# Down-projection of a gated MLP in a transformer block on one core: the weight blocks move to the queue of the left blocks, two buffer pools move, and the results get eight single-bank tiles

## The chip, the cores and the metric

One core of one Trainium2 chip runs the whole program. The metric is the device time of one execution in microseconds (us), the median of three runs. Engines are called PE (TensorE, matmuls), DVE (VectorE), ACT (ScalarE), POOL (GpSimd) and SP (SyncE, which here only issues transfers).

## The reference, cut to what matters

One layer with 1024 tokens and a width of 1024: a token mixer, a layer norm, a gated MLP with a hidden width of 2816, and a second layer norm.

```
def conv_gated_mlp(h, w_up, conv_w, conv_b, w_down):
    u = jnp.einsum('btd,df->btf', h, w_up)
    ...
    uc = conv_b + sum(conv_w[j] * up[:, j:j + T] for j in range(CONV_WIDTH))
    a, v = jnp.split(uc, 2, axis=-1)
    return jnp.einsum('btf,fd->btd', jax.nn.gelu(a) * v, w_down)
...
    h = layer_norm(ALPHA * h + mix, ln1_g[l], ln1_b[l])
    ffn = conv_gated_mlp(h, w_up[l], conv_w[l], conv_b[l], w_down[l])
    h = layer_norm(ALPHA * h + ffn, ln2_g[l], ln2_b[l])
```

## The kernel before, in words

Every large product is made of three matmuls (`mm3`, L83 to L85): each operand is split into a high part, rounded by ACT, and the rest, subtracted by DVE (`split`, L65 and L66). The parts go to buffers of the pool `wp` (five pairs). Both MLP products use a scheme of seven block products in place of eight.

**Up-projection.** `pair(f)` makes the seven products of one pair of filter tiles (f = 0 to 21) in two PSUM units of two banks, `post(f)` the convolution, the gate and the sums of gated blocks, which `store` writes to the DRAM tensors `gd`. Pair j = 10 is the last one (f = 20 and 21). `prep(f)` splits the weights; the split of its block `s1` lies in one pair of tiles `w1h`, `w1l`.

**Down-projection.** `plan` lists 42 steps: seven passes in the order P1, P2, P6, P5, P7, P3, P4, each of NS = 6 steps (five with two row blocks of 128, one with one). A full step is 4 results x 2 blocks x 3 = 24 matmuls of 128x512, a pass is 132. The left operand of step n is a gated block, loaded back from `gd` by `load_a(n)` into one of the three buffers of `rawp` (tile `rawa`, L769, on SP). The right operand is a block of `w_down` or a sum of such blocks. The 24 blocks come in the order of `w_loads` (L847): first those of P1, then those of P2, and so on; `load_w2` (L852) issues four at first and two in each step, on POOL's queue. For P1's first two steps the block goes through `rawp` as well (`rawb`, L797). `prepare(n)` splits both operands; `slot` says where the split goes: to `wp`, or to the three pairs of the second operand pool `dn` (tiles `dh`, `dl`).

P6 builds its right operands in a tile `t2` (L806, one buffer) from blocks changed in place by P2 (L818); L811 and L820 change blocks for later passes. The residual adds ALPHA times the layer norm's output: `residual(t)` loads a stored row block `zd[t]` to a tile `zn` (L857, two buffers), scales it (L858) and adds it to the result `z[t]` (L859). It is called in the passes P5 and P3, and L859 needs what P6 or P7 left in `z[t]`.

Pools on the left side of SBUF are stacked: `bigp` (`bh`, `bl`: operands of the up-projection), `tpp`, then `ugp` (buffers `ca`, `cv` of `post`); `uap` is on the right side. The down-projection's pools take their place: `zq` on the left (weight tiles, `z`, then `zn` and `t2`), `dn` on the right. With `reuse_waits="tile"` a new tile waits for the old tiles under it, without it for all of the old pool. The order of the instructions on each engine is not the written one: the framework plans it, and puts later instructions ahead where it deems earlier ones not yet ready. Slots of one tag are handed out in written order.

Results: `cs` are units of two banks from the same PSUM pool `ps` as before; P1, P6, P7 and P4 add up in `banks[1]` (four results in two units), P2, P5 and P3 in `banks[3]`. `finish` adds them to `z`. In P4 the results 0 and 1 run together, then 2, then 3; `norm2` makes the second layer norm of each row block, in the form "added" with ACT and an accumulating transfer on POOL, in the form "whole" with two DVE instructions of full width (L479, L483).

Of the kernel before, what the change touches and what calls it, by code (L numbers as in the profile page):

```python
# [9 lines left out]
F32 = mybir.dt.float32  # L10
F32R = mybir.dt.float32r
# [6 lines left out]
P = 128  # L18
T = 1024
D = 1024  # L20
# [6 lines left out]
NF = DFF // P  # L27
# [15 lines left out]
def block_kernel(ctx: ExitStack, tc: tile.TileContext, x, xT, w_ct, w_i, pool_w, w_out, w_up, w_down, pk, rows, masks, ident, out):  # L43
    nc = tc.nc
    V, A, G, PE = nc.vector, nc.scalar, nc.gpsimd, nc.tensor

    const = ctx.enter_context(tc.tile_pool(name="const", bufs=1))
    lnp = ctx.enter_context(tc.tile_pool(name="lnp", bufs=1))
    small = ctx.enter_context(tc.tile_pool(name="small", bufs=4))
    rawp = ctx.enter_context(tc.tile_pool(name="rawp", bufs=3))  # L50
    wp = ctx.enter_context(tc.tile_pool(name="wp", bufs=5))
    ps = ctx.enter_context(tc.tile_pool(name="ps", bufs=4, space=bass.MemoryType.PSUM))

    def unit():
        return ps.tile([P, 1024], F32, tag="u", name="u")
# [8 lines left out]
    def split(r, h, l):  # L64
        A.activation(out=h, in_=r, func=AF.Copy)  # L65
        V.tensor_tensor(out=l, in0=r, in1=h.bitcast(F32), op=ALU.subtract)  # L66

    def wpair():
        return wp.tile([P, 1024], F32R, tag="wh", name="wh"), wp.tile([P, 1024], F32R, tag="wl", name="wl")
# [10 lines left out]
    halves, whole = [slice(0, 512), slice(512, 1024)], slice(0, 1024)  # L80
# [293 lines left out]
    for lv in range(NL):  # L374
        G.tensor_copy(out=maskt[:, lv, :].rearrange("p (c t) -> p c t", t=P),
                      in_=mraw[:, lv * P:(lv + 1) * P].rearrange("p (o t) -> p o t", o=1).broadcast_to([P, 4, P]))
# [32 lines left out]
    tmp = [hg.tile([P, 1024], F32, name=f"tmp{j}") for j in range(2)]  # L409
    pb = [tmp[0], sets[0][1], sets[0][2]]  # L410
# [3 lines left out]
    for j in range(4, 16):  # L414
        while len(ahead) < 3 and j + len(ahead) < 16:
            ahead.append(weight(w_ct[j + len(ahead)]))
        w = ahead.pop(0)
# [14 lines left out]
    for h in range(NH):  # L432
        for e in range(2):
# [5 lines left out]
    jps = [(j, j + 1) if j + 1 < NF // 2 else (j,) for j in range(0, NF // 2, 2)]  # L439
    gd = {(n, i): tc.dram_tile([P, len(js), 512], F32, name=f"gd{n}{i}")  # L440
          for n in ("11", "12", "22", "s1", "s2", "s3", "s4") for i, js in enumerate(jps)}
# [14 lines left out]
    def row(i, tag):  # L456
        r = lnp.tile([P, D], F32, tag=tag, name=f"row{i}")
        nc.sync.dma_start(out=r, in_=rows[i:i + 1, :].broadcast_to([P, D]))
        return r
# [26 lines left out]
    def stats(zt, c, st6):  # L486
        V.bn_stats(out=st6[:, c.start // 512, :], in_=zt[:, c])
# [84 lines left out]
    def raw_up(i):  # L572
        if i not in raws:
            raws[i] = raw(w_up[i])
        return raws[i]
# [29 lines left out]
    ua = uap.__enter__()  # L605
    ops, outs = {}, {}
    lo, hi = halves

    def parts(w):
        return [[e[:, c] for e in w] for c in halves]  # L610

    def prep(f):
        ra, rv = raw_up(f), raw_up(NF + f)
        w = wpair()
        split(ra, *w)
        o = ops[f] = {}
        o["11"], o["12"] = parts(w)
        yield


        s1 = ua.tile([P, 512], F32, tag="s1", name="s1")
        V.tensor_tensor(out=s1, in0=rv[:, lo], in1=rv[:, hi], op=ALU.add)
        V.tensor_tensor(out=rv[:, lo], in0=ra[:, lo], in1=rv[:, lo], op=ALU.add)
        yield
        V.tensor_tensor(out=ra[:, lo], in0=s1, in1=ra[:, lo], op=ALU.add)
        V.tensor_tensor(out=ra[:, hi], in0=ra[:, lo], in1=ra[:, hi], op=ALU.add)
        yield
        w = wpair()
        split(ra, *w)
        o["s2"], o["s4"] = parts(w)  # L630
        yield
        w = wpair()
        split(rv, *w)
        o["s3"], o["22"] = parts(w)
        yield
        o["s1"] = [ua.tile([P, 512], F32R, tag=f"w1{n}", name=f"w1{n}", bufs=1) for n in "hl"]
        split(s1, *o["s1"])

    def prod(o, w, b, start, stop):
# [51 lines left out]
    gated = {}  # L691

    def store(n, j, src):
        nc.sync.dma_start(out=gd[n, j // 2][:, j % 2, :], in_=src)

    def post(f):
        a, v = outs.pop(f)
# [30 lines left out]
    def step(gens, n=1):  # L728
        for i in range(n):
            for g in gens:  # L730
                next(g, None)

    preps = [prep(f) for f in range(NF)]
    step(preps[:2])
    norm1(u7, 7, halves)
# [14 lines left out]
    p = post(0)  # L750
# [9 lines left out]
    NS = len(jps)  # L760
# [10 lines left out]
    def w_view(r, q, c):  # L771
        b = w_down[2 * jps[q][0] + r]
        return bass.AP(tensor=b.tensor, offset=b.offset + c.start, ap=[[1024, P], [2 * P * 1024, len(jps[q])], [1, 512]])

    def w_block(r, q, c):
        return ww[r][q][:, :, c]
# [9 lines left out]
    def split2(src, n, k):  # L786
        h, l = [t[:, :k] for t in slot(n)]
        split(src, h, l)
        return h, l

    def prepare(n):
        i, q = plan[n]
        k = len(jps[q])
        a = split2(raw_a.pop(n)[:, :k, :], 2 * n, k)
        if i == P1 and q < 2:
            src = rawp.tile([P, 2, 512], F32, tag="raw", name="rawb")[:, :k]
            nc.sync.dma_start(out=src, in_=w_view(0, q, lo))  # L797
        elif i == P1:
            src = w_block(0, q, lo)
        elif i == P2:  # L800
            src = w_block(1, q, lo)
            w11 = w_block(0, q, lo)
        elif i == P6:
            w21, w22 = w_block(1, q, lo), w_block(1, q, hi)
            src = zq.tile([P, 2, 512], F32, tag="t2", name="t2")[:, :k]
            V.scalar_tensor_tensor(out=src, in0=w_block(0, q, lo), scalar=-1.0, in1=w22, op0=ALU.mult, op1=ALU.subtract)  # L806
        elif i == P5:
            src = w_block(0, q, lo)
        elif i == P7:
            src = w_block(0, q, hi)  # L810
            V.tensor_tensor(out=src, in0=w_block(1, q, hi), in1=src, op=ALU.subtract)  # L811
        elif i == P3:
            src = w_block(1, q, hi)
        else:
            src = w_block(1, q, lo)
        opsd[n] = a, split2(src, 2 * n + 1, k)
        if i == P2:
            V.tensor_tensor(out=w11, in0=w11, in1=w_block(0, q, hi), op=ALU.subtract)  # L818
        elif i == P6:
            V.tensor_tensor(out=w21, in0=w21, in1=src, op=ALU.add)  # L820
# [16 lines left out]
    tpp.__exit__(None, None, None)  # L837
    bigp.__exit__(None, None, None)
    uap.__exit__(None, None, None)
    zq = ctx.enter_context(tc.tile_pool(name="zq", bufs=1, reuse_waits="tile"))  # L840
    dn = ctx.enter_context(tc.tile_pool(name="dn", bufs=3, side="right", reuse_waits="tile"))
    ww = [[zq.tile([P, len(js), D], F32, tag=f"w{r_}{q}", name=f"w{r_}{q}") for q, js in enumerate(jps)] for r_ in range(2)]
    z = [zq.tile([P, D], F32, name=f"z{t}") for t in range(NC)]
    g1, b1_ = row(0, "g"), row(1, "b")
    st6 = maskt[:, 0, :NC * 48].bitcast(F32).rearrange("p (t a b) -> p t a b", a=2, b=6)

# [2 lines left out]

    def load_w2(n):  # L850
        for r_, q, c in w_loads[:n]:
            G.dma_start(out=w_block(r_, q, c), in_=w_view(r_, q, c))  # L852
        del w_loads[:n]

    def residual(t):
        zn = zq.tile([P, D], F32, tag="zn", name="zn", bufs=2)
        nc.sync.dma_start(out=zn, in_=zd[t])  # L857
        V.scalar_tensor_tensor(out=zn, in0=zn, scalar=ALPHA, in1=g1, op0=ALU.mult, op1=ALU.mult)  # L858
        V.tensor_tensor(out=z[t], in0=z[t], in1=zn, op=ALU.add)  # L859

    cs = [unit() for i in range(2)]
    banks = {1: [cs[p // 2][:, halves[p % 2]] for p in range(4)]}
    fresh = {P1: 1, P2: 3, P5: 3, P4: 1}
    where = {P1: 1, P6: 1, P7: 1, P4: 1, P2: 3, P5: 3, P3: 3}

# [34 lines left out]
    def norm2(t, c, how):  # L900
        stats(z[t], c, st6[:, t])
        layer_norm(z[t], g2, b2, st6[:, t], how, out[t * P:(t + 1) * P, :])


    beside = []
    prepared = 1
    load_w2(4)

    def advance(n):
        nonlocal prepared  # L910
        while prepared <= n and prepared < len(plan):
            if prepared not in raw_a:
                load_a(prepared)
            prepare(prepared)
            prepared += 1
            if prepared < len(plan) and prepared not in raw_a:
                load_a(prepared)
            load_w2(2)

    for n in range(6 * NS):  # L920
        i, q = plan[n]
        if n == NS:
            cs += [unit() for e in range(2)]
            banks[3] = [cs[2 + p // 2][:, halves[p % 2]] for p in range(4)]
        advance(n + 1)
        multiply(n, range(4))
        if q == NS - 1:
            for p in range(4):
                finish(i, p)
            if i == P6:  # L930
                beside += [lambda t=t: (residual(t), stats(z[t], lo, st6[:, t])) for t in range(4)]
            elif i == P7:
                beside += [lambda t=t: (residual(t), stats(z[t], hi, st6[:, t])) for t in range(4, 8)]
        elif beside:
            beside.pop(0)()
            if i == P3 and not beside:
                g2, b2 = row(2, "g"), row(3, "b")
# [8 lines left out]
    for q in range(NS):  # L946
        multiply(n0 + q, (2,))
    for p in range(2):
        norm2(4 + p, lo, "added")
    finish(P4, 2)  # L950
    for q in range(NS):
        multiply(n0 + q, (3,))
# [66 lines left out]
```

## Time and profile before

| | |
|---|---|
| median of 3 runs | 1058.08 us (1058.04 to 1058.32) |
| the profiled execution | 1058.64 us, span 1056.6 us, so 2.0 us lie around the span |
| PE busy | 1026.0 us, 97% of the span |
| DVE, ACT, POOL busy | 812.4, 437.8, 62.0 us |
| granted TensorE clock, mean | 0.988 |

Matmuls follow each other every 0.23 us at the full clock, though each record is 0.39 us long (they are pipelined). PE is busy nearly throughout, so the few stretches where it is not are what to look for.

### The profile page before, as it was taken

To read this page: it belongs to the slowest core of one execution; us is meant where nothing else is said; L and a number is where in the kernel's file an instruction comes from. 1 tells how busy PE (TensorE), PEld (TensorE's weight loads), DVE (VectorE), ACT (ScalarE), POOL (GpSimd) and SP (SyncE) were. 2 spreads that over 40 slices of the span, in tenths; PEclk is the share of its full clock that TensorE was granted. 3 is DMA by queue.
4 is the path that set the end of the run, shared out by engine and by line. 5 is a ranking of instruction groups with operands and counts; after the bars stand their busy time and mean duration, and the time that the engine had idled before them with its cause. 6 is when DMAs were issued, how large, how long until landed. Compare 5 with 4: busy or idle time off the path is not lost.

```text
span 1056.6 us, 12003 instructions
## 1 busy us (share of the span) xinstructions
PE 1026.0 (97%) x4680; PEld 839.2 (79%) x4680; DVE 812.4 (77%) x973; ACT 437.8 (41%) x542; POOL 62.0 (6%) x96
## 2 busy tenths in 40 slices
PE   9999999999999999999999999999999399999996
PEld 6888888888888877888778877887877388888884
DVE  6485498967745689988888987987986579795885
ACT  6421453223723375544443444444434233334441
POOL 2000000001100000000000000000000320000033
PEclk9999999999999999999999999999999799999998
DMA  8200211100142223224214323322233982352448
GB/s 323 90 20 1 80 40 41 40 1 20 41 179 100 100 100 120 100 70 140 100 61 139 100 85 115 100 99 102 100 105 133 370 307 82 108 181 98 134 126 239
DMA packets 39944, 118.62 MB, mean 112 GB/s; under 512 B 4432, under 2 KB 5328, under 8 KB 39888
## 3 DMA queue, kind: packets, MB, share of 16 engines
q1 hardware_dynamic: 35680, 103.11, 27.7%
q0 software_dynamic: 4064, 14.68, 4.5%
q8 instruction: 37, 0.61, 0.2%
q14 instruction: 19, 0.16, 0.0%
q10 hardware_dynamic: 144, 0.07, 0.0%
HBM read 89.27 MB, written 28.57 MB: 112 GB/s over the span
## 4 chain that ended last, share of the span: by engine, by line
PE 92%; DVE 3%; DMA 3%; ACT 2%; issue 0%; SPq 0%; POOL 0%; POOLq 0%; DVEq 0%; ACTq 0%
PE u L83 29%; PE u L85 29%; PE u L84 29%; PE u L228 3%; DMA zn<-zd 1%; DMA gd<-ca 1%; PE u L268 1%; PE u L270 1%; PE u L257 1%; DMA hg<-in_xT 1%; ACT hq L520 1%; DMA raw<-in_w_up 1%; DVE wl L66 1%; ACT fh L520 0%; PE u L529 0%
## 5 line engine op out<-in xcount | busy, mean ns | idle before, releaser
L83 PE MATMUL u<-bh,wh 128*128 128x512 f32 x520 | 205.6, 398 | 1.3 <-ACT ua L660 0.7
L84 PE MATMUL u<-bl,wh 128*128 128x512 f32 x520 | 202.9, 390 | 1.0 <-DVE bl L66 1.0
L85 PE MATMUL u<-bh,wl 128*128 128x512 f32 x520 | 202.9, 391 | 0.0
L65 ACT ACTIVATE wh<-raw 128x1024 fp32r<-128x1024 f32 x85 | 88.6, 1057 | 113.1 <-PE u L84 81.3
L66 DVE TENSOR_TENSOR wl<-raw,wh 128x1024 fp32r<-128x1024 f32 x85 | 103.0, 1225 | 25.7 <-ACT wh L65 23.2
L83 PEld LDWEIGHTS u<-bh,wh 128*128 128x128 f32 x520 | 97.6, 188 | 28.1 <-DVE uv L678 5.6
L85 PEld LDWEIGHTS u<-bh,wl 128*128 128x128 f32 x520 | 97.6, 188 | 21.0
L84 PEld LDWEIGHTS u<-bl,wh 128*128 128x128 f32 x520 | 97.7, 188 | 20.8 <-DVE bl L66 1.6
L83 PE MATMUL u<-th,wh 128*128 128x512 f32 x264 | 104.8, 397 | 0.0
L85 PE MATMUL u<-th,wl 128*128 128x512 f32 x264 | 103.3, 391 | 0.8 <-DVE wl L66 0.8
L84 PE MATMUL u<-tlo,wh 128*128 128x512 f32 x264 | 103.3, 391 | 0.0
L65 ACT ACTIVATE wh<-rawa 128x1024 fp32r<-128x1024 f32 (+1 forms) x30 | 30.1, 1002 | 91.6 <-PE u L84 74.9
L83 PEld LDWEIGHTS u<-th,wh 128*128 128x128 f32 x264 | 49.5, 188 | 15.8 <-ACT ua L667 3.2
L85 PEld LDWEIGHTS u<-th,wl 128*128 128x128 f32 x264 | 49.6, 188 | 12.3 <-DVE wl L66 1.2
L83 PE MATMUL u<-wh,bh 128*128 128x512 f32 x144 | 57.8, 401 | 0.0
L84 PEld LDWEIGHTS u<-tlo,wh 128*128 128x128 f32 x264 | 49.6, 188 | 9.7
L687 DVE SCALAR_TENSOR_TENSOR cv<-uv,pkt,cv 128x1023 f32<-128x1023 f32 (+1 forms) x44 | 56.1, 1276 | 0.3 <-ACT cv L685 0.2
L85 PE MATMUL u<-wh,wl 128*128 128x512 f32 x144 | 56.2, 391 | 0.0
L84 PE MATMUL u<-wl,wh 128*128 128x512 f32 x144 | 56.2, 390 | 0.0
L85 PE MATMUL u<-wh,bl 128*128 128x512 f32 x144 | 56.2, 390 | 0.0
L687 DVE SCALAR_TENSOR_TENSOR ca<-ua,pkt,ca 128x1023 f32<-128x1023 f32 (+1 forms) x44 | 56.1, 1276 | 0.0
L83 PE MATMUL u<-wh 128*128 128x512 f32 x144 | 56.1, 390 | 0.0
(216 smaller groups left out, 1978.7 us busy)
## 6 DMA issues: line engine op xcount, KB each, us to landing
raw<-in_w_up SPq DMA_DIRECT2D x42, 512.0 KB, 4.2
w<-in_w_down POOLq DMA_DIRECT2D x20, 512.0 KB, 6.0
rawa<-gds SPq DMA_DIRECT2D x20, 512.0 KB, 3.3
gd<-ca SPq DMA_DIRECT2D x33, 256.0 KB, 2.7
rawa<-gd SPq DMA_DIRECT2D x15, 512.0 KB, 4.6
raw<-in_w_ct SPq DMA_DIRECT2D x13, 512.0 KB, 3.2
gds<-sm SPq DMA_DIRECT2D x22, 256.0 KB, 2.6
gds<-ca SPq DMA_DIRECT2D x22, 256.0 KB, 4.2
```

Of the source, the lines that this page charges most:

```text
L65: A.activation(out=h, in_=r, func=AF.Copy)
L66: V.tensor_tensor(out=l, in0=r, in1=h.bitcast(F32), op=ALU.subtract)
L83: PE.matmul(o, lhsT=ah, rhs=bh, start=start, stop=False, **kw)
L84: PE.matmul(o, lhsT=ah, rhs=bl, start=False, stop=False, **kw)
L85: PE.matmul(o, lhsT=al, rhs=bh, start=False, stop=stop, **kw)
L228: PE.matmul(ul[:, p * P:(p + 1) * P], lhsT=km[:, p * P:(p + 1) * P], rhs=view(QF, p * P + hh, [2 * hh, 64 // hh], [512 - hh, 2], [1, hh]), ...
L257: PE.matmul(up[:, c * P:(c + 1) * P], lhsT=KTr[:, c * P:(c + 1) * P], rhs=vchunk(c, hs), start=True, stop=True)
L268: PE.matmul(uo[:, cs], lhsT=vchunk(c, hs), rhs=sc[:, cs], start=True, stop=c == 0)
L270: PE.matmul(uo[:, cs], lhsT=S[:, (c - 1) * P:c * P], rhs=QF[:, cs], start=False, stop=True)
L520: A.activation(out=o[:, ks], in_=u[:, ks], func=AF.Identity, scale=pkt[:, PK_LN + k:PK_LN + k + 1], bias=pkt[:, PK_LN + KT + k:PK_LN + KT ...
L687: V.scalar_tensor_tensor(out=c[:, 2 - j:], in0=u[:, :T - 2 + j], scalar=pkt[:, cw + j:cw + j + 1], in1=c[:, 2 - j:], op0=ALU.mult, op1=ALU ...
```

## The change

It moves the transfers of the weight blocks (`load_w2`) from POOL's to SP's queue, where they stand behind the `rawa` loads of their step. It moves the seven stores of the last pair (j = 10) from SP's to POOL's queue. The pool `dn` goes to the left side, ahead of `zq`, over the old `bh`. In `zq` the tiles `z` move ahead of the last two weight tiles, and `zn` and `t2` become one tag `tmp` with three buffers. The PSUM pool `ps` is closed, and a new pool `pb`, which waits for all of the old one, gives eight single-bank results. From f = 2 on, the split of `s1` goes to the two tiles `g` and `b` of the pool `lnp` in turn, where the rows `g1`, `b1_` of the first layer norm are loaded afterwards. Row blocks 4 and 5 get the form "whole" of the second layer norm.

```diff
@@ -49,7 +49,8 @@
-    ps = ctx.enter_context(tc.tile_pool(name="ps", bufs=4, space=bass.MemoryType.PSUM))
+    psp = tc.tile_pool(name="psp", bufs=4, space=bass.MemoryType.PSUM)
+    ps = psp.__enter__()
@@ -633,7 +634,11 @@
-        o["s1"] = [ua.tile([P, 512], F32R, tag=f"w1{n}", name=f"w1{n}", bufs=1) for n in "hl"]
+        if f < 2:
+            o["s1"] = [ua.tile([P, 512], F32R, tag=f"w1{n}", name=f"w1{n}", bufs=1) for n in "hl"]
+        else:
+            t = lnp.tile([P, 2, 512], F32R, tag="gb"[f % 2], name="w1")
+            o["s1"] = [t[:, 0, :], t[:, 1, :]]
@@ -691,7 +696,7 @@
-        nc.sync.dma_start(out=gd[n, j // 2][:, j % 2, :], in_=src)
+        (G if j == NF // 2 - 1 else nc.sync).dma_start(out=gd[n, j // 2][:, j % 2, :], in_=src)
@@ -802,7 +807,7 @@
-            src = zq.tile([P, 2, 512], F32, tag="t2", name="t2")[:, :k]
+            src = tmp_tile("t2").rearrange("p (a t) -> p a t", t=512)[:, :k]
@@ -837,10 +842,26 @@
+    psp.__exit__(None, None, None)
+    dn = ctx.enter_context(tc.tile_pool(name="dn", bufs=3, reuse_waits="tile"))
     zq = ctx.enter_context(tc.tile_pool(name="zq", bufs=1, reuse_waits="tile"))
-    dn = ctx.enter_context(tc.tile_pool(name="dn", bufs=3, side="right", reuse_waits="tile"))
-    ww = [[zq.tile([P, len(js), D], F32, tag=f"w{r_}{q}", name=f"w{r_}{q}") for q, js in enumerate(jps)] for r_ in range(2)]
+    pb = ctx.enter_context(tc.tile_pool(name="pb", bufs=1, space=bass.MemoryType.PSUM))
+    place = {}
+
+    def w_tile(r_, q):
+        place[r_, q] = zq.tile([P, len(jps[q]), D], F32, tag=f"w{r_}{q}", name=f"w{r_}{q}")
+
+    def tmp_tile(name):
+        return zq.tile([P, D], F32, tag="tmp", name=name, bufs=3)
+
+    for q in range(NS):
+        w_tile(0, q)
+    for q in range(4):
+        w_tile(1, q)
     z = [zq.tile([P, D], F32, name=f"z{t}") for t in range(NC)]
+    for q in range(4, NS):
+        w_tile(1, q)
+    ww = [[place[r_, q] for q in range(NS)] for r_ in range(2)]
@@ -849,17 +870,16 @@
-            G.dma_start(out=w_block(r_, q, c), in_=w_view(r_, q, c))
+            nc.sync.dma_start(out=w_block(r_, q, c), in_=w_view(r_, q, c))
...
-        zn = zq.tile([P, D], F32, tag="zn", name="zn", bufs=2)
+        zn = tmp_tile("zn")
...
-    cs = [unit() for i in range(2)]
-    banks = {1: [cs[p // 2][:, halves[p % 2]] for p in range(4)]}
+    banks = {i: [pb.tile([P, 512], F32, name=f"c{i}{p}") for p in range(4)] for i in (1, 3)}
@@ -919,9 +939,6 @@
-        if n == NS:
-            cs += [unit() for e in range(2)]
-            banks[3] = [cs[2 + p // 2][:, halves[p % 2]] for p in range(4)]
@@ -946,7 +963,7 @@
-        norm2(4 + p, lo, "added")
+        norm2(4 + p, lo, "whole")
```

## Rows read from the trace of the kernel before

**Rows 1.** The page: granted clock in 40 equal slices of the span.
```profile
PEclk9999999999999999999999999999999799999998
```

**Rows 2.** Windows: stretch, busy us of PE, PEld, DVE, ACT, POOL, clock, DMA share, GB/s.
```profile
30.00:770.00 740.00, 738.39 (x3448) 607.50 (x3447) 581.73 (x712) 318.70 (x412) 18.84 (x36) 1.00 0.24 82
827.10:842.50 15.40, 0.07 (x1) 0.00 (x0) 4.10 (x6) 3.16 (x5) 4.65 (x7) 0.61 1.03 397
842.50:847.40 4.90, 4.89 (x12) 3.83 (x13) 4.90 (x6) 0.00 (x0) 2.41 (x4) 0.50 0.97 332
818.40:866.00 47.60, 31.68 (x127) 25.20 (x127) 28.14 (x30) 16.29 (x18) 16.95 (x24) 0.82 0.98 368
870.00:1020.00 150.00, 150.00 (x656) 122.84 (x655) 122.61 (x131) 58.68 (x64) 0.79 (x2) 1.00 0.37 125
...
1039.10:1046.90 7.80, 7.80 (x33) 6.05 (x33) 3.38 (x4) 0.02 (x1) 2.51 (x3) 1.00 0.95 226
```

**Rows 3.** Waits of PE: waiting line, awaited line, us in total, times, longest.
```profile
PE u L84 <- DVE dl L66: 15.3, 1, 15.3
```

**Rows 4.** Chain that ended last, in order of time (start us, us, what).
```profile
827.08 7.46 DMA gd<-ca
834.62 7.85 DMA zn<-zd
842.51 0.80 PE u L84
```

**Rows 5.** Timeline of DVE (start us, us, instruction, in brackets the idle time before).
```profile
817.74 0.69 DVE L681 TENSOR_TENSOR ua<-u,ua 128x512 f32<-128x512 f32 x1 [0.20 <-PE u L85]
...
828.18 0.69 DVE L725 TENSOR_TENSOR ca<-sm,ca 128x512 f32<-128x512 f32 x1
840.10 1.22 DVE L858 SCALAR_TENSOR_TENSOR zn<-zn,row 128x1024 f32<-128x1024 f32 x1 [11.23 <-DMA zn<-zd]
841.24 1.22 DVE L66 TENSOR_TENSOR dl<-w,dh 128x1024 fp32r<-128x1024 f32 x1
```

**Rows 6.** Timeline of ACT.
```profile
825.34 1.04 ACT L65 ACTIVATE dh<-w 128x1024 fp32r<-128x1024 f32 x1
```

**Rows 7.** Timeline of PE.
```profile
809.29 0.39 PE L84 MATMUL u<-wl,wh 128*128 128x512 f32 x1
...
826.43 0.73 PE L83 MATMUL u<-dh,wh 128*128 128x512 f32 x2 [0.57 <-ACT dh L65]
...
855.58 0.40 PE L83 MATMUL u<-wh 128*128 128x512 f32 x1
...
863.79 0.40 PE L83 MATMUL u<-dh,wh 128*128 128x512 f32 x1
...
869.41 0.40 PE L83 MATMUL u<-dh 128*128 128x512 f32 x1
```

**Rows 8.** Transfers: lines' issues (ns, first and last start), landing times, timeline of SP.
```profile
L852 POOL DMA_DIRECT2D w<-in_w_down x24: 567/724/978, 818.4 to 861.0; - x24
...
w<-in_w_down POOLq DMA_DIRECT2D x20, 512.0 KB, 6.0
rawa<-gd SPq DMA_DIRECT2D x15, 512.0 KB, 4.6
...
816.37 7.05 SPq L769 DMA_DIRECT2D rawa<-gd  x3
...
L458 SPq DMA_DIRECT2D row<-in_rows x4: 328/330/333, 401.1 to 1002.5; - x4
```

**Rows 9.** Timeline of PE, DVE and SP at the end.
```profile
1039.03 0.51 PE L83 MATMUL u<-p,p 128*128 128x512 f32 x1 [0.78 <-DVE z L880]
...
1042.11 1.28 DVE L483 SCALAR_TENSOR_TENSOR z<-z,rs,row 128x1024 f32<-128x1024 f32 x1 [0.77 <-POOL rs L464]
1046.93 0.69 DVE L880 TENSOR_TENSOR z<-z,u 128x512 f32<-128x512 f32 x1 [3.54 <-PE u L85]
...
1050.57 3.19 SPq L484 DMA_DIRECT2D out<-z  x4
```

## The prediction

> **What bounds the kernel now.** I read the page first: of its 40 slices only the 32nd (819 to 845 us) and the last have a lowered clock [rows 1]. The windows then say where PE loses time. From 30 to 770 us it is busy 738.39 of 740 us, from 870 to 1020 all of 150: nothing can be won there. Between 827.1 and 842.5 us it does nothing, and in the 4.9 us behind that it runs at a granted clock of 0.50, the 1.2 GHz level of its two [rows 2]. The waits of PE name one wait of 15.3 us, for DVE's `dl` [rows 3].
>
> That `dl` is the low part of the right operand of step 2 in P1. ACT had its high part by 826.4 us [rows 6], so the weight block was there. DVE was free after L725, at 828.9, but the next instruction in its queue is L858, the scaling of a residual that is wanted two passes later. It stands 11.23 us for its `zn`; the split behind it starts at 841.24 and PE goes on at once [rows 5, 7]. The chain shows why `zn` is late: its load shares 16 busy transfer engines (DMA share 0.98, 368 GB/s, from 818.4 to 866) with the 24 weight blocks [rows 2], and its second tile lies on a buffer whose store had to land first [rows 4].
>
> **The change, part by part.** *One tag for `t2` and `zn`.* P6's six `t2` come first in the written order, so `zn` gets a slot only when P6's splits release one. It could not be otherwise: a `zn` is freed by L859, which needs P6's result, which needs `t2`. So L858 can no longer stand in P1, and the 15.3 us wait loses its cause. The two scalings move to P5, 2.3 us more for DVE in a stretch where it has 150 − 122.6 = 27.4 us free [rows 2]: nothing on the path.
>
> *Eight banks in a new PSUM pool.* P1 may start only when the last reader of the old pool, L681, is done: 817.74 + 0.69 = 818.43 [rows 5], so P1 starts at about 818.5. Before, matmuls of P1's first step filled gaps in the last pair, from 809.29 on for instance [rows 7]; I count 12 of them. That filling is lost, whatever else happens, and is the price of this edit.
>
> *The sum for P1.* 60 matmuls of P1 and P2 run from 855.58 to 869.41, 0.2305 us each [rows 7]. A pass is 132: 30.4 us. Undisturbed, P1 runs from 818.5 to 848.9, and P2 starts there; before, it started at 863.79 [rows 7]. Gain 14.9 us. The same from its parts: 15.6 us between 826.9 and 842.5, 0.7 us of waiting just before, 2.4 us of slow clock (82 matmuls took 842.51 to 863.79, 21.28 us, for 18.9 at full rate), less 12 x 0.23 = 2.8 us of lost filling and 0.96 us from 817.54 to 818.5.
>
> *What is late next.* PE wants step 2 at 818.5 + 48 x 0.2305 = 829.6. If the split follows L725 in DVE's queue, it ends at 828.9 + 1.22 = 830.1: a wait of 0.5 us; if it goes ahead of L707, none. The upper end: the block's transfer behind the last left block that SP sent early (816.37 + 7.05 = 823.4), landing after 6.0 us as on POOL's queue [rows 8], then ACT 1.04 and DVE 1.22: 831.7, a wait of 2.1. I take 0.4, nearest to the rows of DVE. After a wait of 0.78 us on PE the granted clock is 1.00 [rows 2, 9], so I charge no clock for it.
>
> *Weight blocks on SP.* 24 issues of 0.57 to 0.98 us leave POOL [rows 8]; it did nothing that PE waited for. On SP they stand among the left blocks. If they keep the written order, two behind each left block, the left block of P2's first step has 7.1 MB before and with it; at 368 GB/s it lands 19 us after 818.4, at 838, with all six stores of the last post (1.6 MB, on the other queue) at 842. Its split must begin at 848.9 − 2.3 = 846.6. Later steps gain on that, since a step moves 1.5 MB, 4.3 us, and PE takes 5.5. So nothing; what it costs if the order is another is the second rival.
>
> The Trainium skill, DMA: Bandwidth & Descriptors, section "Issuing engines are not separate DMA queues", speaks against expecting anything from the other queue: it only saves the sequencer's time. By it this edit alone is worth zero, which agrees with the zero I use; the rows above show the engines full in any case.
>
> *Stores of the last pair on POOL.* Seven issues of at most 0.98 us on an empty engine, landing after some 6 us; the block "12" that is read first of the six is wanted more than 10 us later, in P2's last step. The "11" stored near 809 lands by 816, ahead of SP's load of it. Nothing.
>
> *`w1` in two buffers, rows loaded later.* PE has 1.6 us idle in all the up-projection up to 770 [rows 2], so a second buffer gains at most that; I take 0. The rows of the layer norm, loaded at 401 us before [rows 8], now wait for the last `s1` product (about 806) and are wanted at 848.9 first: 40 us cover it. *`dn` on the left* is free when PE leaves `bh` at about 817.5: nothing, with no loss as bound.
>
> *The tail.* Before, the matmuls of result 3 waited for DVE's reading of result 2, in the same unit: PE idle from 1038.08 to 1039.03 [rows 9], 0.95 us, which single-bank results remove. "Whole" for blocks 4 and 5 adds two DVE instructions of 1.28 us [rows 9]. Their cover is the 3.54 us in which DVE waited for the last matmul, 0.95 less now: 2.6 of 2.56. Just enough; without cover up to 2.6 us, I take 0. On the other side, the last stores of SP left from 1050.57 on, close behind one that had waited for an accumulating transfer [rows 9]: between 0 and 1 us, I take 0.
>
> Sum: 14.9 − 0.4 + 0.95 = 15.4 us. The profiled execution of 1058.64 us becomes 1043.2; the median of the runs lies 0.56 us below it, so 1042.7.
>
> **The rivals.** *Left blocks land behind a flood of weights.* Most weight tiles are free at 817.5, and the planner puts what is ready first: `zn` stood two passes too early [rows 5]. If all 24 blocks go ahead of step 7's left block (20 of 512 KB, four of half that: 11.5 MB), they need, with three and a half left blocks and the stores, 14.9 MB, 40.5 us at 368 GB/s. The block lands at 858.9, its split ends at 861.2, and PE wanted it at 848.9 + 5.5 = 854.4. That is 6.8 us, and 2.4 us more of slow clock if it falls as it did at 842.5: gain 6.2, time 1051.9; half a flood gives some 1047. For it: the planner's habit. Against: the left blocks are earlier in the written order, and DVE frees their buffers one by one from 816 on [rows 8].
>
> The same page, section "Queues, rings and completion order", has each transfer engine take turns between the queues that have work, and keep order inside one. By that rule the left blocks had every other turn before and lose it now; the landing of 4.6 us beside the weights' 6.0 is no contradiction. It would make this rival likelier than its rows alone.
>
> *The stall stays.* If some `zn` still runs in P1, PE resumes at 842.5 again, 0.95 us is won in the tail and 0.5 lost, since 84 matmuls are left then where there were 82: about 1057.6, no difference. Against it stands the dependence above.
>
> *Slower: another early DVE instruction takes the place of L858.* L806 needs the first block of the last group, the 19th. It lands after 9.2 MB of weights, 1.3 of left blocks and 1.6 of stores, 12.1 MB, 33 us after 818.4: at 851.3. If L806 stands ahead of the split of step 2, PE resumes after both, at 853.7; 84 matmuls and 2.4 us of slow clock end P1 at 875.5, 11.7 us later than before, and the tail gives 0.95 back: 1069. It decides from where the awaited data lands after 842. For it: the same planner. Against: before, the splits of P1 all came ahead of such work, except for `zn`, which depended on nothing in the pass.
>
> *More than forecast: the filling is not lost.* If the pool's wait falls on each bank by itself, the 3.7 us come back: 1039.
>
> **How the numbers follow.** This kernel's measurement can tell about 0.2%, 2.1 us, from no change. Chances: forecast (1040.5 to 1045) 0.62, flood in part or whole (1045 to 1052) 0.22, stall stays 0.05, slower 0.05, more than forecast 0.06. Faster is 0.62 + 0.22 + 0.06 = 0.90, same 0.05, slower 0.05. The range leaves out the two cases without gain, the upper end of the flood and the best case: 1040 to 1050.5.
>
> **What would show it.** Right: no L858 ahead of P5; P2's first matmul near 849; no `u<-wh` matmuls inside the last pair, but three gaps of 1 to 1.6 us there; clock 1.00 between 827 and 860; no idle PE before result 3 in the tail. Wrong: a long wait of PE for a split that waits for `rawa` (flood), or for DVE behind L806, L818 or L858; a lowered clock anywhere in P1 or P2; DVE busy without a gap when the last matmul ends.

## The result, and the profile after

| | before | after |
|---|---|---|
| median | 1058.2 us (1058.04 to 1058.59) | 1047.2 us (1045.23 to 1047.6) |
| the profiled execution | 1058.64 us, span 1056.6 | 1047.6 us, span 1045.5 |
| granted clock, mean | 0.988 | 0.994 |

The ratio is 0.9892, with a 95% interval of 0.9875 to 0.9909: faster by 11 us. The forecast was 1042.7 in a range of 1040 to 1050.5. The gain is there, 4.4 us smaller than the sum made it, and the sum's parts are off by more than that, in both directions.

In the code after the change the lines of the functions named below are 1 to 21 higher: the split is L66 (ACT) and L67 (DVE), the three matmuls L84 to L86, the last reader of the old PSUM pool L686 (L681 before), `load_a` L774, the weight loads L873, the residual L878 to L880, and results are called `c`.

First the page's slices of the granted clock, and windows with the columns of [rows 2]:

```profile
PEclk9999999999999999999999999999999999999998
```

```profile
818.00:825.00 7.00, 6.43 (x28) 5.37 (x29) 5.78 (x6) 3.35 (x4) 0.00 (x0) 1.00 0.27 95
...
829.70:834.90 5.20, 0.00 (x1) 0.00 (x0) 0.00 (x0) 1.08 (x2) 0.00 (x0) 0.92 0.97 331
834.90:840.90 6.00, 5.93 (x13) 4.24 (x14) 5.05 (x5) 4.08 (x5) 0.00 (x0) 0.50 1.05 403
...
1029.20:1036.80 7.60, 7.60 (x34) 5.98 (x32) 4.70 (x6) 0.00 (x0) 1.88 (x2) 1.00 0.88 329
```

The slice that was dented before [rows 1] is not dented now, but the stretch of the old stall still holds a smaller one, which the slices hide: a digit 9 stands for 90% or more, and slices 32 and 33 (810.3 to 836.4 to 862.5 us) have 0.95 and 0.91. The windows show it: PE does nothing from 829.7 to 834.9 and then runs 6 us at 0.50, the 1.2 GHz level. The first window shows something that the forecast had excluded: from 818 to 825 the transfer engines are hardly used, a share of 0.27. In the kernel before it was 0.88 in the same 7 us:

```profile
818.00:825.00 7.00, 7.00 (x32) 5.81 (x31) 6.28 (x6) 3.40 (x4) 3.74 (x5) 1.00 0.88 296
```

The waits of PE (columns as in [rows 3]) and the tile `zn`:

```profile
PE c L84 <- ACT dh L66: 5.2, 1, 5.2
PE u L84 <- DVE uv L680: 1.4, 1, 1.4
PE c L84 <- ACT wh L66: 0.9, 1, 0.9
PE u L84 <- DVE uv L683: 0.8, 1, 0.8
```

```profile
L878 SPq DMA_DIRECT2D zn<-zd x7: 319/320/426, 895.5 to 932.5; - x7
L879 DVE SCALAR_TENSOR_TENSOR zn<-zn,row x7: 1208/1216/1218, 900.8 to 938.1; 128x1024 f32<-128x1024 f32 x7
```

The old wait for DVE's `dl` [rows 3] is gone, and no scaling of `zn` starts before 900.8. The last three waits are the gaps around the last pair that the new PSUM pool was said to leave; two of them are under the 1 to 1.6 us that were forecast. The 5.2 us are new: step 2 of P1 waits for ACT's part of its weight block. The chain, in order of time, says why (start us, us, what):

```profile
823.36 1.07 ACT ca L710
...
825.59 1.23 DVE wl L67
826.84 0.32 SPq L774
827.21 6.59 DMA w<-in_w_down
833.82 1.06 ACT dh L66
834.93 1.22 PE c L84 x2
```

Read it from below. PE waited for ACT, ACT for the weight block, and the block was sent only at 827.21, behind the load of a left block on SP (L774). That load waited for a buffer, until DVE had split what lay in it, and that split stood behind the work on the last pair, the gelu L710 first. The first weight load left at 818.4 before [rows 8]. SP's timeline shows what follows it:

```profile
816.37 10.79 SPq L774 DMA_DIRECT2D rawa<-gd  x3
827.21 15.32 SPq L873 DMA_DIRECT2D w<-in_w_down  x14
843.56 0.34 SPq L774 DMA_DIRECT2D rawa<-gd  x1
```

Fourteen weight blocks in a row go ahead of the next left block, which is the flood of the prediction's rivals. No PE wait comes of it here: after 834.93 the list above has none. PE's timeline marks P1's first matmul, P2's, and P2's second step (as in [rows 7]); the last fence is DVE and SP at the end (as in [rows 9]):

```profile
818.57 0.47 PE L84 MATMUL c<-wh 128*128 128x512 f32 x1 [0.88 <-ACT wh L66]
...
857.08 0.39 PE L84 MATMUL c<-dh,wh 128*128 128x512 f32 x1
...
862.52 0.39 PE L84 MATMUL c<-dh 128*128 128x512 f32 x1
```

```profile
1036.85 0.69 DVE L900 TENSOR_TENSOR z<-z,c 128x512 f32<-128x512 f32 x1 [2.08 <-PE c L86]
...
1041.20 1.30 SPq L485 DMA_DIRECT2D out<-z  x3
```

A step of 24 matmuls takes 5.44 us (857.08 to 862.52), for 5.62 before (863.79 to 869.41 [rows 7]). So three stretches divide the difference, and they are used for every kernel below: from the last reading of the old pool (L681 or L686) to P2's first matmul, from there to the end of the last matmul, and from there to the end of the span. All are differences of starts and ends in the timelines; what lies ahead of the first one differs by up to 2 us from run to run (the last reading starts between 816.98 and 818.97 in the fourteen profiled executions), and the only part of the change in it, the second buffer for `w1`, leaves no trace there beyond that spread. Each ratio is to runs of the kernel before on the same chip. The stretches are those of one profiled execution; for the kernel before with the weights on SP it lay near the lowest of its times (1049.2 to 1053.5).

| kernel | median us | ratio to before, 95% interval | to P2 | P2 to last matmul | tail |
|---|---|---|---|---|---|
| before | 1058.2 | | 46.05 | 183.1 | 9.7 |
| after | 1047.2 | 0.9892 (0.9875 to 0.9909) | 39.35 | 179.7 | 8.7 |
| after, weights on POOL | 1049.6 | 0.9922 (0.9903 to 0.9940) | 41.75 | 179.7 | 8.2 |
| after, stores on SP | 1047.9 | 0.9913 (0.9899 to 0.9926) | 39.38 | 179.7 | 8.3 |
| after, both moves undone | 1039.9 | 0.9820 (0.9807 to 0.9834) | 31.05 | 179.8 | 8.3 |
| after, four weights on POOL, stores on SP | 1039.0 | 0.9814 (0.9801 to 0.9827) | 31.05 | 179.7 | 9.0 |
| after, own tags | 1046.3 | 0.9882 (0.9867 to 0.9898) | 38.04 | 180.4 | 8.3 |
| after, `dn` on the right | 1050.4 | 0.9922 (0.9909 to 0.9934) | 39.62 | 182.0 | 8.7 |
| before, common tag | 1044.9 | 0.9871 (0.9856 to 0.9886) | 32.56 | 183.1 | 8.3 |
| before, weights on SP | 1052.9 | 0.9946 (0.9931 to 0.9961) | 38.41 | 183.1 | 8.9 |
| before, `dn` on the left | 1056.5 | 0.9984 (0.9975 to 0.9992) | 45.67 | 180.8 | 10.3 |
| before, common tag and `dn` on the left | 1043.2 | 0.9867 (0.9853 to 0.9880) | 32.63 | 180.9 | 9.6 |
| four weights on POOL, `dn` behind `zq` | 1039.6 | 0.9831 (0.9818 to 0.9844) | 31.04 | 179.7 | 9.0 |
| four weights on POOL, two-bank results | 1042.8 | 0.9862 (0.9849 to 0.9876) | 31.07 | 182.6 | 8.9 |

### The profile page after: what moved, and what is told of

Its sections match the earlier page's. It is cut to its first block, busy times and chain, and to the rows that moved or that the text cites. A ratio compares the mean times of both kernels' runs of the same rounds, so it can differ in the third digit from the quotient of the medians.

```text
span 1045.5 us, 11991 instructions
## 1 busy us (share of the span) xinstructions
PE 1023.3 (98%) x4680; PEld 839.0 (80%) x4680; DVE 815.0 (78%) x975; ACT 434.3 (42%) x540; POOL 49.2 (5%) x77
## 4 chain that ended last, share of the span: by engine, by line
PE 90%; DVE 4%; DMA 2%; ACT 2%; issue 1%; SPq 0%; POOL 0%; POOLq 0%; DVEq 0%; ACTq 0%
PE u L84 22%; PE u L85 21%; PE u L86 21%; PE c L85 6%; PE c L84 6%; PE c L86 6%; PE u L229 3%; DMA raw<-in_w_up 1%; DVE wl L67 1%; PE u L269 1%; DMA w<-in_w_down 1%; PE u L271 1%; PE u L258 1%; DMA hg<-in_xT 1%; ACT fh L521 0%
## 5 line engine op out<-in xcount | busy, mean ns | idle before, releaser
L84 PE MATMUL u<-bh,wh 128*128 128x512 f32 x520 | 206.0, 398 | 2.8 <-DVE uv L683 1.6
L86 PE MATMUL u<-bh,wl 128*128 128x512 f32 x520 | 202.5, 390 | 0.0
L66 ACT ACTIVATE wh<-raw 128x1024 fp32r<-128x1024 f32 x85 | 88.3, 1057 | 88.6 <-PE u L85 67.6
L84 PEld LDWEIGHTS u<-bh,wh 128*128 128x128 f32 x520 | 97.6, 188 | 30.7 <-DVE uv L683 8.1
L67 DVE TENSOR_TENSOR wl<-raw,wh 128x1024 fp32r<-128x1024 f32 x85 | 102.6, 1221 | 25.2 <-ACT wh L66 22.8
L86 PEld LDWEIGHTS u<-bh,wl 128*128 128x128 f32 x520 | 97.6, 188 | 20.8
L84 PE MATMUL u<-th,wh 128*128 128x512 f32 x264 | 104.8, 397 | 2.2 <-DVE uv L680 2.2
L86 PE MATMUL u<-th,wl 128*128 128x512 f32 x264 | 102.9, 390 | 0.0
L84 PEld LDWEIGHTS u<-th,wh 128*128 128x128 f32 x264 | 49.5, 188 | 18.1 <-DVE uv L680 4.9
L66 ACT ACTIVATE wh<-rawa 128x1024 fp32r<-128x1024 f32 (+1 forms) x30 | 30.1, 1002 | 70.3 <-PE c L85 40.6
L86 PEld LDWEIGHTS u<-th,wl 128*128 128x128 f32 x264 | 49.6, 188 | 10.9
L84 PE MATMUL u<-wh,bh 128*128 128x512 f32 x144 | 57.8, 401 | 0.0
L84 PE MATMUL c<-wh 128*128 128x512 f32 x144 | 56.1, 390 | 0.9 <-ACT wh L66 0.9
L86 PE MATMUL u<-wh,bl 128*128 128x512 f32 x144 | 56.2, 390 | 0.0
L85 PE MATMUL u<-wl,bh 128*128 128x512 f32 x144 | 56.1, 390 | 0.0
L85 PE MATMUL c<-wl,wh 128*128 128x512 f32 x144 | 56.0, 389 | 0.0
## 6 DMA issues: line engine op xcount, KB each, us to landing
w<-in_w_down SPq DMA_DIRECT2D x20, 512.0 KB, 10.1
```

Of the source, the lines that this page charges most:

```text
L84: PE.matmul(o, lhsT=ah, rhs=bh, start=start, stop=False, **kw)
L85: PE.matmul(o, lhsT=ah, rhs=bl, start=False, stop=False, **kw)
L86: PE.matmul(o, lhsT=al, rhs=bh, start=False, stop=stop, **kw)
```

## The experiments

**The queues.** Theory: the 5.2 us are the price of the first weight load's place behind an instruction that waits. Four kernels make a square of the two queue moves (weights, and stores of the last pair), and a fifth refines one corner. First the weights alone back on POOL:

```diff
-            nc.sync.dma_start(out=w_block(r_, q, c), in_=w_view(r_, q, c))
+            G.dma_start(out=w_block(r_, q, c), in_=w_view(r_, q, c))
```

> The kernel after with the weight loads back on POOL's queue, all else kept. Theory (the 5.2 us wait at 829.7 and the slow clock behind it come from the first weight load standing behind a left block's load on SP, which waits for a split): the first load leaves near 818.4, PE waits under 1 us for step 2, no clock of 0.50 in P1, P2's first matmul near 849 for 857.08, so about 8 us less than the kernel after: 1038.5 to 1040.5. Rival A (the transfer engines are full in any case, the queue only changes who issues): 1045 to 1048. Rival B (left blocks suffer from the weights on another queue): a PE wait for a split of rawa in P1 or P2, 1042 to 1050.

It took 1049.6 us: the expectation failed, and no late left block was the cause, as its second rival had it. Waits of PE, and POOL's timeline:

```profile
PE c L84 <- ACT dh L66: 8.1, 1, 8.1
```

```profile
825.91 1.07 POOL L699 DMA_DIRECT2D gd<-ca  x2 [9.90 <-DVE ca L712]
...
829.10 0.54 POOL L699 DMA_DIRECT2D gds<-ca  x1 [0.19 <-issue]
829.77 0.74 POOL L873 DMA_DIRECT2D w<-in_w_down  x1
```

What I had left out is that the change also put the last pair's stores on POOL. They wait 9.90 us for DVE, and the weight loads stand behind them. So the theory needed its other half: no queue is good or bad, the load must not stand behind *anything* that waits. That predicts the two corners left. Both moves undone:

```diff
-            nc.sync.dma_start(out=w_block(r_, q, c), in_=w_view(r_, q, c))
+            G.dma_start(out=w_block(r_, q, c), in_=w_view(r_, q, c))
...
-        (G if j == NF // 2 - 1 else nc.sync).dma_start(out=gd[n, j // 2][:, j % 2, :], in_=src)
+        nc.sync.dma_start(out=gd[n, j // 2][:, j % 2, :], in_=src)
```

> The kernel after with both queue moves undone: weight loads on POOL, the stores of the last pair on SP, so that no weight load stands behind anything that waits. Theory (the 5.2 us wait for step 2 and the slow clock behind it are the price of the place in the queue alone): the first weight load leaves near 818.5, ACT's part of step 2's block is done near 826.8, PE waits 0.5 to 1 us for DVE's split behind the last sums of the post (830.4), no clock of 0.50, P2's first matmul near 849.5, 179.7 us from there to the last matmul, 8.4 us of tail: 1039 to 1040.5. Rival A (a late left block takes its place, with the weights on a queue of their own): 1042 to 1048. Rival B (the queues make no difference): 1046 to 1048.

It took 1039.9 us, as expected; the wait of 0.5 to 1 us for DVE's split did not come. POOL's and ACT's timelines, and two windows:

```profile
818.74 3.01 POOL L873 DMA_DIRECT2D w<-in_w_down  x4 [425.26 <-PE u L86]
```

```profile
826.21 1.04 ACT L66 ACTIVATE dh<-w 128x1024 fp32r<-128x1024 f32 x1
```

```profile
825.00:830.00 5.00, 5.00 (x23) 4.14 (x23) 4.54 (x6) 5.00 (x6) 2.07 (x3) 1.00 0.92 333
830.00:835.00 5.00, 5.00 (x23) 3.88 (x23) 5.00 (x6) 1.25 (x3) 2.01 (x3) 1.00 1.02 370
```

The loads leave as soon as PE has left the tiles' old contents, step 2's block is split in time, PE has no gap and the clock stays at 1.00. The last corner keeps the weights on SP and moves only the stores back:

```diff
-        (G if j == NF // 2 - 1 else nc.sync).dma_start(out=gd[n, j // 2][:, j % 2, :], in_=src)
+        nc.sync.dma_start(out=gd[n, j // 2][:, j % 2, :], in_=src)
```

> The kernel after with the last pair's stores back on SP, the weight loads left on SP: the fourth corner of the square of the two queue moves. Theory (a weight load leaves when everything ahead of it in its queue has left): it stands behind the six stores of the last post, which wait for DVE until 828 to 830, so the first load leaves 1 to 3 us later than in the kernel after (827.21), PE's wait for step 2 grows from 5.2 to 6 to 8 us: 1047 to 1050. Rival (the corner with the stores on SP is the good one, whatever queue the weights use): 1039 to 1041.

1047.9 us, as expected. PE's wait, then SP's timeline, with stores and left block ahead of the first weight load:

```profile
PE c L84 <- ACT dh L66: 6.2, 1, 6.2
```

```profile
827.43 0.32 SPq L774 DMA_DIRECT2D rawa<-gd  x1
...
829.49 0.32 SPq L699 DMA_DIRECT2D gds<-ca  x1
829.85 12.04 SPq L873 DMA_DIRECT2D w<-in_w_down  x14
```

So the first load leaves at 818.74, 827.21, 829.77 and 829.85 in the four corners, and PE waits for it 0, 5.2, 8.1 and 6.2 us. It landed 5.5 us after 829.85 and 6.9 after 829.77, which is most of why the last two differ. Next, only the first four blocks on POOL, the rest on SP:

```diff
-            nc.sync.dma_start(out=w_block(r_, q, c), in_=w_view(r_, q, c))
+            (G if r_ == 0 and c is lo and q > 1 else nc.sync).dma_start(out=w_block(r_, q, c), in_=w_view(r_, q, c))
```

(and the stores on SP, as above.)

> The kernel after with the first four weight blocks alone on POOL's queue, the other twenty on SP's, and the last pair's stores back on SP. Theory (only the place of the first blocks counts): as with all weights on POOL, 1039 to 1040.5. Rival (ten weight blocks in a row on SP ahead of the next left block delay P2's second step): a PE wait for a split of rawa near 855, 1041 to 1046.

1039.0 us, no wait for step 2 and none near 855, although ten weight blocks in a row leave SP ahead of P2's second left block. PE's timeline gives P1's third step and P2's first matmul, 31.05 us behind L686 as in the corner with both moves undone; the last fence is SP's ten blocks and DVE's split of that left block, done at 850.09, 3.4 us before PE takes it up at 853.53:

```profile
828.84 0.39 PE L84 MATMUL c<-dh,wh 128*128 128x512 f32 x1
...
848.09 0.39 PE L84 MATMUL c<-dh,wh 128*128 128x512 f32 x1
```

```profile
828.63 7.98 SPq L873 DMA_DIRECT2D w<-in_w_down  x10
...
848.86 1.23 DVE L67 TENSOR_TENSOR dl<-rawa,dh 128x1024 fp32r<-128x1024 f32 x1 [1.25 <-ACT dh L66]
```

The twenty others may stand on either queue. This version beats both kernels: 1.9% faster than before.

**What took `zn` out of P1.** The prediction gave it to the common tag. First the tag alone, on the kernel before:

```diff
-            src = zq.tile([P, 2, 512], F32, tag="t2", name="t2")[:, :k]
+            src = zq.tile([P, 2, 512], F32, tag="tmp", name="t2", bufs=3)[:, :k]
...
-        zn = zq.tile([P, D], F32, tag="zn", name="zn", bufs=2)
+        zn = zq.tile([P, D], F32, tag="tmp", name="zn", bufs=3)
```

> The kernel before with one edit: t2 and zn share one tag of three buffers. Theory (the tag alone takes the scaling of zn out of P1, and with it the 15.3 us wait and the slow clock behind it; the weight blocks stay on POOL's queue and leave from 818.4, so step 2's block lands in time): gain 15.6 + 2.4 us less a wait of 0 to 0.5, so 1040.0 to 1041, P2's first matmul near 846, no PE wait over 1 us in P1. Rival A (without the move of the weights to SP the left blocks or the weights land late and another wait takes its place): 1045 to 1053. Rival B (the stall needs the other edits to go): 1057 to 1059.

1044.9 us: these two lines alone give as much as the whole change (a ratio of 0.9871 against 0.9892; the intervals overlap). P2 came later than expected. The scaling of `zn`, which starts at 897.3, the wait of PE, and a window with the clock at 0.66:

```profile
L858 DVE SCALAR_TENSOR_TENSOR zn<-zn,row x7: 1201/1212/1216, 897.3 to 932.7; 128x1024 f32<-128x1024 f32 x7
```

```profile
PE u L84 <- DVE dl L66: 2.9, 1, 2.9
```

```profile
830.00:835.00 5.00, 4.50 (x14) 3.61 (x15) 5.00 (x6) 0.70 (x2) 2.01 (x3) 0.66 1.04 406
```

PE begins step 2 at 826.88, after 0.57 us of waiting, does two matmuls and stands 2.89 us for a split that comes behind the last sums of the post in DVE's queue. The expected 0 to 0.5 forgot that the kernel before reaches this step 3 us earlier than the one after. Now the reverse, the kernel after with tags as before:

```diff
-            src = tmp_tile("t2").rearrange("p (a t) -> p a t", t=512)[:, :k]
+            src = zq.tile([P, 2, 512], F32, tag="t2", name="t2")[:, :k]
...
-        zn = tmp_tile("zn")
+        zn = zq.tile([P, D], F32, tag="zn", name="zn", bufs=2)
```

> The kernel after with zn and t2 on tags of their own, as before. Theory of the prediction (the tag is what keeps L858 out of P1): the wait of some 15 us comes back, 1055 to 1062. Rival (the weight loads on SP's queue keep zn's load, and with it the scaling, out of P1 as well): no zn in P1, the same 5.2 us wait for step 2 as in the kernel after, 1045 to 1048.

The rival holds: 1046.3 us. The tile `zn`, and PE's wait:

```profile
L879 DVE SCALAR_TENSOR_TENSOR zn<-zn,row x6: 1199/1214/1224, 882.8 to 937.4; 128x1024 f32<-128x1024 f32 x6
```

```profile
PE c L84 <- ACT dh L66: 5.1, 1, 5.1
```

No scaling before 882.8, with its own buffers free from the start. The weight loads on SP alone, on the kernel before:

```diff
-            G.dma_start(out=w_block(r_, q, c), in_=w_view(r_, q, c))
+            nc.sync.dma_start(out=w_block(r_, q, c), in_=w_view(r_, q, c))
```

> The kernel before with one edit: the weight loads on SP's queue (tags as before, the last pair's stores on SP too). Theory (zn's load now stands behind the weights in SP's queue, so its scaling leaves P1 without the tag; but the first weight load stands behind the last pair's stores too, and leaves near 830): step 2's block on ACT near 837.5, PE idle from 827 to 838, 3 us of slow clock, P2's first matmul near 860: 1053 to 1056. Rival A (the tag is needed): 1057 to 1062. Rival B (the queue alone gives all of the change's gain): 1046 to 1049.

1052.9 us, at the edge of what was expected (PE resumed at 834.14 rather than near 838). `zn`'s scaling leaves P1 here too, and a wait for the weights takes its place:

```profile
L858 DVE SCALAR_TENSOR_TENSOR zn<-zn,row x6: 1215/1224/1229, 881.1 to 937.3; 128x1024 f32<-128x1024 f32 x6
```

```profile
PE u L83 <- ACT dh L65: 9.0, 1, 9.0
```

So either edit removes the old stall; the tag does it for 2.9 us of a new wait, the queue for 9.0.

**The place of `dn`.** The step of 5.44 us was not in the forecast. The kernel after with `dn` on the right:

```diff
-    dn = ctx.enter_context(tc.tile_pool(name="dn", bufs=3, reuse_waits="tile"))
+    dn = ctx.enter_context(tc.tile_pool(name="dn", bufs=3, side="right", reuse_waits="tile"))
```

> The kernel after with the second operand pool dn back on the right side, all else kept. Theory (the place of dn sets the spacing of the matmuls that take one operand from wp and one from dn: 0.234 us before, 0.2267 after): the spacing of those 216 matmuls goes back to 0.234 us, between P2's start and the last matmul 1.6 to 2.4 us more, 1048.5 to 1050. Rival (the closer spacing comes from the traffic of the transfers or from the single-bank results): spacing stays at 0.227, time within 0.7 us of the kernel after, 1045 to 1048.

And the kernel before with `dn` on the left, ahead of `zq`:

```diff
+    dn = ctx.enter_context(tc.tile_pool(name="dn", bufs=3, reuse_waits="tile"))
     zq = ctx.enter_context(tc.tile_pool(name="zq", bufs=1, reuse_waits="tile"))
-    dn = ctx.enter_context(tc.tile_pool(name="dn", bufs=3, side="right", reuse_waits="tile"))
```

> The kernel before with one edit: the second operand pool dn on the left side, ahead of zq. Theory (the place of dn alone sets the spacing of matmuls with one operand from wp and one from dn): such a step of 24 takes 5.44 us for 5.62, and 2.3 us go between P2's first and the last matmul; the 15.3 us wait stays; 2 to 3 us less than the kernel before. Rival (the place counts only together with the single-bank results): no difference, within 0.7 us.

1050.4 (0.4 over the theory's range) and 1056.5 us: 3 us lost, 2 gained, and from P2 to the last matmul 2.3 us each way, whatever results and queues there are. PE's groups by shape from 870 to 1000 us show it in the recorded length of a matmul, first for `dn` on the right in the kernel after, then on the left in the kernel before:

```profile
L84 PE MATMUL c<-dh,wh 128*128 128x512 f32 x48 | 19.0, 397 | 0.0
```

```profile
L83 PE MATMUL u<-dh,wh 128*128 128x512 f32 x48 | 18.7, 389 | 0.0
```

Is it the distance from `wp`? In the version with four blocks on POOL, `dn` went behind `zq`:

```diff
-    dn = ctx.enter_context(tc.tile_pool(name="dn", bufs=3, reuse_waits="tile"))
     zq = ctx.enter_context(tc.tile_pool(name="zq", bufs=1, reuse_waits="tile"))
+    dn = ctx.enter_context(tc.tile_pool(name="dn", bufs=3, reuse_waits="tile"))
```

> The version with four weight blocks on POOL's queue (1039.0), with dn still on the left side but behind zq, so some 130 KB per partition away from wp. Theory (the distance of the two operands is what counts, not the side): a step of 24 with one operand from wp and one from dn takes 5.62 us again, 2.3 us more: 1041 to 1042. Rival (only the place at the far right end is bad): 5.44 us, 1038.5 to 1040.

```profile
L84 PE MATMUL c<-dh,wh 128*128 128x512 f32 x56 | 21.8, 389 | 0.0
```

1039.6 us and 389 ns: the distance theory falls, as far as the written order gives the place (the addresses themselves were not read). What makes the right side slow stays open.

**The lost filling and the single banks.** The kernel before with tag and `dn` (both diffs above) keeps the old PSUM pool, and with it the matmuls of P1 inside the last pair:

> The kernel before with two edits: the common tag of t2 and zn, and dn on the left. It keeps the old PSUM pool, so the matmuls of P1 that fill the gaps of the last pair. Theory (the filling is worth nothing, because PE then stands longer before DVE's split of step 2, which ends near 830.4 either way; what the single banks add is the 0.95 us of the tail and the 1 to 1.3 us of slow clock behind that longer stand): a wait of about 2.9 us at step 2, 1041.5 to 1043. Rival (the filling is worth its 3.8 us, as the prediction charged it): 1035 to 1038.

1043.2 us, just above the theory's numbers and far from the rival's. PE waits as with the tag alone:

```profile
PE u L84 <- DVE dl L66: 2.9, 1, 2.9
```

To P2 it takes 32.63 us, and 31.05 without the filling. Last, the version with four blocks on POOL with two-bank results:

```diff
-    banks = {i: [pb.tile([P, 512], F32, name=f"c{i}{p}") for p in range(4)] for i in (1, 3)}
+    cs = [pb.tile([P, 1024], F32, name=f"c{e}") for e in range(4)]
+    banks = {i: [cs[i - 1 + p // 2][:, halves[p % 2]] for p in range(4)] for i in (1, 3)}
```

> The version with four weight blocks on POOL's queue (1039.0), with the eight results as halves of four tiles of two banks in the new pool. Theory (single banks are worth the wait of PE for DVE's reading of result 2 in the tail): PE stands 0.8 to 0.95 us before result 3, nothing else moves: 1039.8 to 1040.2. Rival (that wait is hidden by what DVE does next anyway): 1038.5 to 1039.3.

1042.8 us, more than either side expected. DVE's timeline, then PE's (L901 is L900 of the kernel after):

```profile
1022.17 1.29 DVE L484 SCALAR_TENSOR_TENSOR z<-z,rs,row 128x1024 f32<-128x1024 f32 x1 [0.46 <-POOL rs L465]
1023.37 0.68 DVE L901 TENSOR_TENSOR z<-z,c 128x512 f32<-128x512 f32 x1
```

```profile
1024.11 0.50 PE L84 MATMUL c<-p,p 128*128 128x512 f32 x1 [1.97 <-DVE z L901]
```

With blocks 4 and 5 in the form "whole", DVE reads result 2 behind two more instructions (L484), and PE waits 1.97 us where the kernel before waited 0.78 [rows 9]. Since the records of matmuls overlap, what counts is the distance of their starts: 2.36 us before this one (1021.75 to 1024.11) and 0.34 behind it, where 0.2267 is usual, so 2.24 us are lost. A wait of 0.38 us for a split, at 1008, costs 0.65 in the same way; the version with own tags has that wait too, so it need not come of the banks. Together they are 2.89 of the 2.95 us.

## Why the prediction was right, and where it was not

*The old stall.* Right in the mechanism: L858 leaves P1, PE's 15.3 us wait goes. "The 15.3 us wait loses its cause" through the tag is shown by the tag alone. It was not the only edit of the change to do so: the weights' queue does it too. One reason that the prediction gave for the late `zn` did not count, the second tile's wait for a store [rows 4]. DVE stood for the first tile, whose load left at 829.8 and landed 10.3 us later; the second tile was scaled only behind the splits:

```profile
846.99 1.21 DVE L858 SCALAR_TENSOR_TENSOR zn<-zn,row 128x1024 f32<-128x1024 f32 x1
```

*The new pool.* P1 was to start at about 818.5 and did at 818.57 (the trace names ACT's split that ended there as what PE waited for; the last reader of the old pool was done at 818.42). An undisturbed P1 was to take 30.4 us; with four blocks on POOL it took 30.21 (817.88 to 848.09). But the 3.8 us charged for the filling seem to have been no cost: with it PE stands 2.9 us before the split of step 2 and then runs at a lowered clock, without it (both moves undone) it does neither and reaches P2 1.5 us sooner. The versions compared differ in other parts of the change too, so that the filling itself is worth nothing is argued, not shown; by the same comparison the rival "the filling is not lost", at 1039, had nothing to give.

*What is late next: the step that failed.* It gave step 2 a wait of 0.4 us, with 2.1 as upper end, and charged "no clock". It was 5.2 us, and the two steps behind it took 13.99 us (834.93 to 848.92) where 48 matmuls at 0.2267 take 10.88: 3.1 us of slow clock. P2 began at 857.08 for 849.3, 7.8 us late. The upper end took SP's last left block from the trace of before, gone by 823.4 [rows 8]; in the kernel after it waits until 826.84, because the split of the buffer's contents now comes behind the gelu. The prediction priced the moved issues ("24 issues of 0.57 to 0.98 us leave POOL", "So nothing") and named the queue, but did not ask what each instruction *ahead* of the first weight load waits for. Its reason for a zero was that the engines are full in any case; with the loads held back they were at 0.27 from 818 to 825. It leaned there on the Trainium skill (DMA: Bandwidth & Descriptors, section "Issuing engines are not separate DMA queues"), which states that starting transfers on several engines only saves the time on the sequencer. On how busy the transfer engines get the traces agree: a share of 1.02 with the weights on POOL (830 to 835 us, both moves undone) and of 1.05 on SP (834.9 to 840.9, kernel after). But what stood ahead in the issuing engine's queue decided when the first load left, and undoing that gave 7 to 8 us (1039.9 and 1039.0 for 1047.2). By the prediction's own list of signs this was "a lowered clock anywhere in P1 or P2", one of those for wrong; the range held all the same.

*The flood.* Fourteen blocks in a row did leave SP, and PE waited for none of the left blocks. The kernel after is no test of it, since PE came to P2's second left block only at 862.52; ACT's split of that block began at 853.69, and on the forecast's times it was wanted at 854.4. The version with ten blocks in a row and P2 at 848.09 is the test, and there was no wait. That "half a flood gives some 1047", the time measured, is chance: the delay was of a weight, not of a left block. The time lies in the part of the range that was there for this rival, so that the range held is luck too.

*`dn` on the left,* "nothing, with no loss as bound", is mis-sized: 2.3 us gained, of the 2.4 that P2 to the end came out better than the sum.

*The tail.* The 0.95 us of single banks came: PE is busy 7.60 of 7.60 us around result 3. The cover for "whole" held with 2.08 us to spare, where the sum left next to none. From the last matmul to the end it took 8.7 us for 9.7; 0 to 1 was the bound and zero the choice. In nine executions with "whole" this stretch is 8.2 to 9.0, in five with "added" 8.3 to 10.3. The two ranges overlap, and the form alone was not tested.

*The other zeros.* The second buffer for `w1` moved nothing that can be seen: the last reading of the old PSUM pool starts at 817.73 for 817.74 before. The stores on POOL cost nothing while the weights are on SP (1047.2, and 1047.9 with the stores on SP), but with the weights behind them on POOL they are what holds these back (1049.6 for 1039.9).

So 1043.2 + 7.8 − 2.4 − 1.0 = 1047.6, the profiled execution. A miss of 7.8 us on one wait was covered for 3.4 us by two gains that nobody had forecast.

## What to carry to other kernels

Before a transfer is moved to another queue, list what will stand ahead of its *first* issue there and what each of those waits for; one load that waits for a buffer, or one store that waits for a result, holds back all that is behind it, while the transfer engines are hardly used (a share of 0.27 here). Where a wait is removed, look for the next one in the changed order rather than in the times of before. And where PE is the bound, compare the spacing of its matmuls between groups of operands: 3% on 216 of the 792 matmuls behind P2's start was 1.6 of the 2.3 us.

## What the runs showed of the hardware that was not expected

- Matmuls with one operand from `wp` and one from `dn` follow each other every 0.234 us with `dn` on the right (5.62 us for 24) and every 0.2267 on the left (5.44), in all kernels here; with both operands from one pool a full step takes 5.44 to 5.49 us in the first case and 5.44 in the second. Which property of the place does it is open.
- What a stand of PE cost in slow clock did not grow with its length. Against the spacing at full clock, what was left of P1 took 1.4 us more after a stand of 2.9 us (clock 0.66 from 830 to 835), 1.9 after 5.1 (own tags), 3.1 after 5.2 (the kernel after, 0.50 for 6 us), 2.2 after 6.2, 2.6 after 8.1, 2.0 after 9.0 and 2.4 after 15.3 (0.50 for 4.9 us [rows 2]). What makes the two stands of 5.1 and 5.2 us differ is open.
- With fourteen loads in a row on SP, a block of 512 KB landed 10.1 us after its issue (median of all on that queue), for 6.0 on POOL's queue before [rows 8], and between 815 and 850 us SP itself stood 8.9 us, eight times, for earlier blocks to land. No wait of PE was seen to come of it.
